# Cosine-similarity attention: reciprocal norms by a GpSimd power instead of Newton steps on VectorE

## The chip, the cores and the metric

One core of a Trainium2 chip. The metric is the device time of one run in microseconds (us), lower is better. Engines: PE (matrix products), DVE (VectorE), ACT (ScalarE), POOL (GpSimd), SP (issues DMAs). A difference of about 0.2% can be told from none.

## The reference

Eight batches of twelve heads, 512 tokens of 64 numbers each. Q and K are divided by their row norms, the scores are divided by tau = 0.1, and softmax weights multiply V.

```python
Q_norm = Q / (np.linalg.norm(Q, axis=-1, keepdims=True) + 1e-10)
K_norm = K / (np.linalg.norm(K, axis=-1, keepdims=True) + 1e-10)
scores = np.einsum('bhqd,bhkd->bhqk', Q_norm, K_norm) / tau
weights = np.exp(scores - np.max(scores, axis=-1, keepdims=True))
weights = weights / (np.sum(weights, axis=-1, keepdims=True) + 1e-10)
return np.einsum('bhqk,bhkd->bhqd', weights, V)
```

## The kernel before, in words

The 96 heads are taken as 48 pairs s = 0 to 47. Each operation is a node with a key, an engine, the nodes it needs and a function that issues it. `ORDER` lists, for each of the five engines, the keys in the order in which the engine issues them; the engines run these lists strictly in order and wait for one another by semaphores. So a node that waits holds up all that stand behind it on its engine. A key such as `SCL.4.1` is pair 4's product for K (0 is Q, 1 is K).

For a pair s the work is:

- `LD.s.0`, `LD.s.1`, `LV.s` (L379, L382): SP loads Q, K and V, 256 KB each, into rings of 18 (Q, K) and 6 (V) buffers. The first three K loads are on ACT's queue.
- `SQ.s.0` (L231): POOL squares Q and K together, 128x1024 in one instruction, into bf16. Pairs 0 to 2 are split between POOL and ACT.
- `SSQ.s` (L246) and `RED.s` (L253): PE adds groups of four columns by a product with the identity, DVE adds the rest. For eight pairs (`DIRECT`) DVE reduces the squares itself (L240).
- `NEW.g.k` (L349 to L368): pairs 2 and 3 are groups g of their own, from pair 4 on a group is two pairs. DVE works out the reciprocal norms from a bit-trick seed (L350) by two Newton steps: two times L341 and L342, and three times the form of L346, the last two for Q's and for K's result. That is eight instructions on at most 32 columns. The tiles are in PSUM (`nps`) and SBUF (`ys`, `rk`).
- `SCL.s.0` on DVE and `SCL.s.1` on POOL (both L270): Q and K times their reciprocal norms, 128x512 each, into bf16 `qn`. K of pairs 2 and 3 is on DVE.
- `TR.s` (L277) on PE turns `qn`, `EVA.s` (L421) on DVE copies it to `qt`. For seven pairs (`XT`) a DMA turns the K half (L416).
- `SCO.s.c` (L431), c = 0 to 3: scores of 128 keys by 512 queries for two heads, into one of two halves of `scps`. `SCO.s.c` waits until the exponential two steps back has read its half.
- `EXP.s.c` (L453): ACT takes the exponential of 128x1024 scores; since the norms are 1, no maximum is subtracted. Pair 0 has halves with a scale of its own (L443).
- `VC.s` (L458): POOL turns V into bf16, with a column of ones beside it.
- `PV.s.h.t` (L469), `RCP.s` (L481), `NRM.s` (L483), `ST.s` (L487): PE multiplies the weights by V, DVE divides by the sums, SP stores 256 KB. The last pair is done in three parts (L498 to L517).

Pairs 0 and 1 get their reciprocal norms from ACT (`LN`, `EX`, L259 and L263). `warm` and `fill` are matrix products without use that keep PE busy at the start (L218).

Of the kernel before, what the change touches and what calls it, by code (L numbers as in the profile page):

```python
# [5 lines left out]
ALU = mybir.AluOpType  # L6
# [119 lines left out]
def bass_cosine_similarity_attention_kernel(  # L126
# [12 lines left out]
    MAGIC = float(0x5F375A86)  # L139
    f32, bf16, i32 = mybir.dt.float32, mybir.dt.bfloat16, mybir.dt.int32  # L140
# [5 lines left out]
    def sb(name, shape, dt):  # L146
        return nc.alloc_sbuf_tensor(name, shape, dt)
# [11 lines left out]
    rk = [sb(f"rk{i}", [128, W], f32) for i in range(R_X)]  # L159
# [41 lines left out]
    def scores_read(s, c):  # L201
# [9 lines left out]
        compare_op=ALU.is_equal, fill=0.0))  # L211
    P.add("vone", "pool", ["eye"], lambda e: e.memset(  # L212
# [110 lines left out]
    def k_norms(g, i, j):  # L323

        tile = n_ps[:, g % R_X, 5 * W : 6 * W] if engine("pool", "SCL", first[g] + i, 1) == "dve" else rk[g % R_X][:, :]
        return tile[:, 8 * i : 8 * j]

    def k_runs(g):

        engs = [engine("pool", "SCL", first[g] + i, 1) for i in range(sizes[g])]  # L330
        cuts = [0] + [i for i in range(1, sizes[g]) if engs[i] != engs[i - 1]] + [sizes[g]]
        return list(zip(cuts, cuts[1:]))

    def norms(g):

        pairs = range(first[g], first[g] + sizes[g])
        m = 8 * sizes[g]
        xg = n_ps[:, g % R_X, 0 : 2 * m]
        tg = n_ps[:, g % R_X, 2 * W : 2 * W + 2 * m]
        yg = ys[g % R_X][:, 0 : 2 * m]  # L340
        yx = lambda e: e.tensor_tensor(out=tg, in0=xg, in1=yg, op=ALU.mult)  # L341
        yyx = lambda e: e.scalar_tensor_tensor(  # L342
            out=tg, in0=tg, scalar=-0.5, in1=yg, op0=ALU.mult, op1=ALU.mult)

        def up(dst, lo, hi):
            return lambda e: e.scalar_tensor_tensor(  # L346
                out=dst, in0=tg[:, lo:hi], scalar=1.5, in1=yg[:, lo:hi], op0=ALU.add, op1=ALU.mult)
# [7 lines left out]
        for k, step in enumerate(steps):  # L355
            if k:
                needs = [("NEW", g, k - 1)]
            else:
                needs = [("RED", i, w) for i in pairs for w in range(2) if ("RED", i, w) in P.ops]
            if k < 2:  # L360
                needs += [n for n in (("NEW", g - R_X, j) for j in range(6, 11)) if n in P.ops]
            if k == 6 and g >= R_X:
                needs += [("SCL", i, 0) for i in range(first[g - R_X], first[g - R_X] + sizes[g - R_X])]
            P.add(("NEW", g, k), "dve", needs, step)
        for k, (i, j) in enumerate(k_runs(g), 7):
            P.add(("NEW", g, k), "dve",
                  [("NEW", g, 5)] + ([("SCL", p, 1) for p in range(first[g - R_X], first[g - R_X] + sizes[g - R_X])] if g >= R_X else []),
                  up(k_norms(g, i, j), m + 8 * i, m + 8 * j))  # L368

    def pair(s):  # L370
# [55 lines left out]
        for c in range(NT):  # L426
            b = c % 2

            def sco(e, c=c, b=b):
                for h in range(2):  # L430
# [6 lines left out]
                  [("SCO", s, c - 1) if c else None, ("EVA", s), key("EVA", s, 1), key("XT", s),  # L437
# [99 lines left out]
ON = {'SQ.0.0.0': 'pool', 'SQ.0.0.1': 'act', 'SQ.0.1': 'act', 'SCL.0.1': 'pool', 'EVA.0.1': 'dve', 'SQ.1.0': 'pool', 'SQ.1.1': 'act', 'SCL.1.1': 'pool', 'SQ.2.0': 'pool', 'SQ.2.1': 'act', 'SCL.2.1': 'dve', 'SCL.3.1': 'dve'}  # L537
# [174 lines left out]
```

## Time and profile before

| | |
|---|---|
| Median of three runs | 194.41 us (194.25 to 194.46) |
| Span of the profiled execution, first to last instruction | 192.3 us |
| What the median has outside that span | 2.1 us |
| TensorE clock granted, mean | 0.995 |
| Exponentials of 128x1024 on ACT | 187, mean 1135 ns, overlapping |
| DMA moved | 51.71 MB, mean 269 GB/s |

For the profiled execution the profile gives the span; its own total time is not listed, so it is set against the runs by the difference in the third row. In the profile, a row such as "L270 POOL TENSOR_TENSOR ... x44 | 45.6, 1046 | 10.2" is a group of 44 instructions of line 270 on POOL, busy 45.6 us together, 1046 ns each, with 10.2 us of idle time ahead of them and behind the arrow what ended most of it. Rows of a timeline begin with the start and the length in us. A DMA row ends with the size and the us from issue to landing; one that comes from a narrow window has only the issue in that window.

### The profile page before, as it was taken

How to read it: one execution, taken by the hardware profiler on the slowest of the kernel's cores; microseconds unless marked ns; L12 is line 12 of the kernel's file. 1: busy time of each engine (PE TensorE's matmuls, PEld its weight loads, DVE VectorE, ACT ScalarE, POOL GpSimd, SP SyncE). 2: the span in 40 equal slices, each digit the busy share in tenths (PEclk: the TensorE clock that was granted, in tenths of full speed). 3: DMA queues.
4: the chain of work that ended last, by engine and by line, in shares of the span. 5: the costliest groups of instructions: out<-in, count | busy, mean ns of one | idle time of the engine just before them, and what ended most of it. 6: DMA issues, size and time to landing. Idle time of an engine off the chain costs nothing.

```text
span 192.3 us, 7111 instructions
## 1 busy us (share of the span) xinstructions
PE 179.5 (93%) x2944; PEld 117.6 (61%) x2944; DVE 148.3 (77%) x450; ACT 182.3 (95%) x210; POOL 161.8 (84%) x149
## 2 busy tenths in 40 slices
PE   7799999999998999999999899999999999999891
PEld 5466666656665565666666565666566656566560
DVE  1588887988888798868897887798888778976632
ACT  3599999999999999999999999999999999999990
POOL 4599899999999969999989988799999999927000
PEclk9999999999999999999999999999999999999998
DMA  5999999999999999989999999038799536650545
GB/s 185 360 349 349 352 336 321 373 251 344 341 376 303 374 364 332 314 251 310 364 346 339 285 376 387 16 88 254 242 254 356 130 109 197 193 136 3 182 148 165
DMA packets 56240, 51.71 MB, mean 269 GB/s; under 512 B 6928, under 2 KB 56208, under 8 KB 56208
## 3 DMA queue, kind: packets, MB, share of 16 engines
q1 hardware_dynamic: 55248, 50.41, 84.6%
q10 hardware_dynamic: 960, 0.85, 1.3%
q8 instruction: 23, 0.38, 0.9%
q14 instruction: 9, 0.07, 0.1%
HBM read 37.75 MB, written 12.58 MB: 262 GB/s over the span
## 4 chain that ended last, share of the span: by engine, by line
ACT 67%; POOL 15%; PE 8%; DMA 3%; DVE 2%; issue 2%; SPq 0%
ACT et L453 67%; POOL sq L231 8%; POOL qn L270 4%; DMA qk<-in_Q_dram 3%; POOL vb L458 3%; PE scps L431 2%; PE ops L469 2%; PE xps L246 2%; PE ops L218 1%; PE xps L277 1%; DVE ob L513 1%; PE nps L498 0%; SPq L294 0%; DVE ob L483 0%; POOL vb L212 0%
## 5 line engine op out<-in xcount | busy, mean ns | idle before, releaser
L453 ACT ACTIVATE et<-scps 128x1024 bf16<-128x1024 f32 x187 | 172.2, 1135 | 0.3
L231 POOL TENSOR_TENSOR sq<-qk 128x1024 bf16<-128x1024 f32 (+2 forms) x48 | 87.5, 1837 | 4.2 <-DMA qk<-in_Q_dram 4.2
L431 PE MATMUL scps<-qt 64*128 64x512 bf16 x384 | 74.7, 386 | 4.4 <-ACT et L453 2.4
L469 PEld LDWEIGHTS ops<-vb,et 128*128 128x128 bf16 x1504 | 53.4, 98 | 27.2 <-issue 22.2
L469 PE MATMUL ops<-vb,et 128*128 128x65 bf16 x1504 | 68.2, 194 | 0.6 <-DVE nps L341 0.4
L270 POOL TENSOR_TENSOR qn<-qk,rk 128x512 bf16<-128x512 f32 x44 | 45.6, 1046 | 10.2 <-DVE rk L346 10.2
L421 DVE COPY qt<-xps 128x1024 bf16<-128x1024 bf16 (+1 forms) x47 | 30.4, 647 | 3.7 <-PE xps L277 3.2
L483 DVE TENSOR_TENSOR ob<-ops,rd 128x512 f32<-128x512 f32 x47 | 32.4, 689 | 1.1
L270 DVE TENSOR_TENSOR qn<-qk,nps 128x512 bf16<-128x512 f32 x48 | 31.9, 680 | 0.3
L431 PEld LDWEIGHTS scps<-qt 64*128 64x128 bf16 x384 | 18.6, 92 | 20.3 <-ACT et L453 7.4
L458 POOL TENSOR_SCALAR vb<-vf 128x512 bf16<-128x512 f32 x48 | 29.7, 630 | 0.0
L277 PE MATMUL xps<-ident,qn 128*128 128x128 bf16 x352 | 27.9, 220 | 0.4 <-DVE qn L270 0.2
L246 PE MATMUL xps<-sq,ident 128*128 128x64 bf16 x624 | 24.9, 192 | 2.0 <-POOL sq L231 0.9
L277 PEld LDWEIGHTS xps<-ident,qn 128*128 128x128 bf16 x352 | 19.9, 98 | 10.4 <-issue 3.0
L246 PEld LDWEIGHTS xps<-sq,ident 128*128 128x128 bf16 x624 | 20.8, 97 | 8.9 <-issue 3.8
L481 DVE RECIPROCAL rd<-ops 128x8 f32<-128x8 f32 x47 | 9.7, 206 | 15.6 <-PE ops L469 15.2
L253 DVE TENSOR_REDUCE nps<-xps 128x16 f32<-128x64 f32 x38 | 8.8, 232 | 9.3 <-PE xps L246 8.9
L240 DVE TENSOR_REDUCE nps<-sq 128x8 f32<-128x512 bf16 x16 | 10.8, 684 | 0.0
L341 DVE TENSOR_TENSOR nps<-nps,ys 128x32 f32<-128x32 f32 (+1 forms) x48 | 9.3, 195 | 1.1
L342 DVE SCALAR_TENSOR_TENSOR nps<-nps,ys 128x32 f32<-128x32 f32 (+1 forms) x48 | 9.2, 193 | 1.0
L218 PE MATMUL scps<-warm_in 128*128 128x256 bf16 x28 | 5.8, 384 | 1.1 <-DVE warm_in L216 1.1
L218 PEld LDWEIGHTS scps<-warm_in 128*128 128x128 bf16 x28 | 3.7, 138 | 2.3 <-DVE warm_in L216 1.1
(42 smaller groups left out, 46.1 us busy)
## 6 DMA issues: line engine op xcount, KB each, us to landing
vf<-in_V_dram SPq DMA_DIRECT2D x48, 256.0 KB, 6.0
qk<-in_Q_dram SPq DMA_DIRECT2D x47, 256.0 KB, 6.0
out_dram<-ob SPq DMA_DIRECT2D x47, 256.0 KB, 5.3
qk<-in_K_dram SPq DMA_DIRECT2D x45, 256.0 KB, 6.0
qk<-in_K_dram ACTq DMA_DIRECT2D x3, 256.0 KB, 4.7
qk<-in_Q_dram SPq DMA_DIRECT2D x2, 128.0 KB, 2.7
out_dram<-ob SPq DMA_DIRECT2D x1, 128.0 KB, 2.3
qt<-qn SPq DMA_TRANSPOSE x7, 4.9
```

Source lines behind the costliest of these rows:

```text
L218: P.add(key, "pe", needs, lambda e: e.matmul(out=bank[:, 0:256], lhsT=warm_in[:, 0:128], rhs=warm_in[:, :], start=True, stop=True))
L231: emit = lambda e: e.tensor_tensor(out=b, in0=a, in1=a, op=ALU.mult)
L240: lambda e, w=w: e.tensor_reduce(out=dst(w), in_=sq[s % R_SQ][:, 8 * w : 8 * w + 8, :], axis=AX.X, op=ALU.add))
L246: last = e.matmul(out=x_ps[:, 0:64], lhsT=ident[:, :], rhs=sq[s % R_SQ][:, :, 4 * k : 4 * k + 4], start=(k == 0), stop=(k == 15))
L270: lambda e: e.tensor_tensor(out=qn[iqn][:, w].rearrange("p t h d -> p h t d"), in0=qk[iq][:, w].rearrange("p h (t d) -> p h t d", t=NT), i ...
L277: last = e.transpose(dst[:, i, :], qn[s % R_QN][:, b // NT, b % NT].rearrange("p h d -> p (h d)"), ident[:, :])
L421: lambda e: e.tensor_copy(out=qt[iqt][:, :].rearrange("p w t x -> p (w t) x")[:, 0:nb], in_=tb[:, 0:nb]))
L431: last = e.matmul(out=sc_ps[:, 2 * b + h, :], lhsT=qt[iqt][64 * h : 64 * h + 64, 1, c, :], rhs=qt[iqt][64 * h : 64 * h + 64, 0, :, :], sta ...
L453: lambda e, c=c, b=b: e.activation(out=et[iet][:, c, :, :], in_=sc_ps[:, 2 * b : 2 * b + 2, :], func=ACT.Exp, scale=inv_tau))
L458: lambda e: e.tensor_scalar(out=vb[:, iq, :, :, 0:DIM].rearrange("p c h d -> p h c d"), in0=vf[iv][:, :, :].rearrange("p h (c d) -> p h c ...
L469: last = e.matmul(out=o_ps[:, h, 65 * t : 65 * t + 65], lhsT=et[iet][:, c, h, 128 * t : 128 * t + 128], rhs=vb[:, iq, c, h, :], start=(c = ...
L483: lambda e: e.tensor_tensor(out=ob[io][:, :], in0=grid[:, :, :, 0:DIM], in1=rd[io][:, :].unsqueeze(3).to_broadcast([128, 2, NT, DIM]), op= ...
```

## The change

Four things change.

1. The Newton steps go. A group's sums are clamped from below by DVE into SBUF (`NEW.g.0`), POOL raises them to the power -0.5 in one instruction of at most 32 columns (`POW.g`, against a column of -0.5), and DVE copies the result to PSUM (`NEW.g.1`). The products of the group on DVE need the copy, a K product on POOL needs the power alone.
2. K's product of the odd pairs from 5 to 47 goes from POOL to DVE. Those of pairs 4, 6, and so on to 46 stay on POOL.
3. The order lists of all five engines are others.
4. The `fill` products get fixed places in their own chain: they are added ahead of the pairs, `SCO.0.1` names the ninth and the first `PV` the last of them. They run in PE's order, which the order list sets.

```diff
-        steps = [
-            lambda e: e.tensor_scalar(
-                out=yg.bitcast(i32), in0=xg.bitcast(i32), scalar1=-0.5, scalar2=MAGIC,
-                op0=ALU.mult, op1=ALU.add),
-            yx, yyx, up(yg, 0, 2 * m), yx, yyx,
-            up(n_ps[:, g % R_X, 4 * W : 4 * W + m], 0, m)]
...
+        P.add(("NEW", g, 0), "dve", needs + [key("POW", g - R_X)],
+              lambda e: e.tensor_scalar(out=yg, in0=xg, scalar1=TINY, scalar2=1.0, op0=ALU.max, op1=ALU.mult))
...
+        P.add(("POW", g), "pool", [("NEW", g, 0), "half", key("NEW", g - R_X, 1)] + gone,
+              lambda e: e.tensor_tensor(out=rg, in0=yg, in1=half[:, 0:1].to_broadcast([128, 2 * m]), op=ALU.pow))
...
+        P.add(("NEW", g, 1), "dve", [("POW", g)] + old,
+              lambda e: e.tensor_copy(out=n_ps[:, g % R_X, 2 * W : 2 * W + n], in_=rg[:, 0:n]))
...
+            rk, done = k_norms(g, i)
+            scaled(s, 0, "dve", n_ps[:, g % R_X, 2 * W + c8 : 2 * W + c8 + 8], [("NEW", g, 1)])
+            scaled(s, 1, engine("pool", "SCL", s, 1), rk, [done])
```

The first part of the orders, as far as the prediction speaks of it (the rest differs in the same way):

```diff
 "sp"
-        LD.0.0.0 LD.0.0.1 LD.1.0 LD.2.0 LV.0 LD.3.1 LD.3.0 LD.4.1 LD.4.0 LD.5.1 LD.5.0 LD.7.1 LV.1 LD.6.1 LD.6.0 LD.9.0
-        LD.7.0 LD.8.1 LV.2 LD.11.0 LV.4 LD.8.0 LD.13.1 LD.9.1 LV.3 LD.11.1 LV.6 LV.5 LV.7 LD.10.1 LV.8 LD.10.0 LD.17.0
-        LD.15.1 LD.16.1 LD.12.1 LD.13.0 LD.12.0 LD.14.1 ST.0 LD.18.0 LV.9 LD.14.0 LD.15.0 LD.16.0 LD.25.0 XT.9 ST.3
+        LD.0.0.0 LD.0.0.1 LD.1.0 LD.2.0 LV.0 LD.3.1 LD.4.0 LD.3.0 LD.9.1 LD.4.1 LD.9.0 LD.5.0 LD.6.0 LD.7.1 LD.5.1 LV.1
+        LD.6.1 LV.2 LD.10.0 LV.5 LV.3 LD.7.0 LD.11.0 LD.14.1 LD.8.0 LD.16.0 LD.8.1 LD.11.1 ST.0 LD.15.0 LV.4 LD.13.1
+        LD.14.0 LV.8 LD.10.1 LV.6 LD.15.1 LD.25.0 LV.9 LD.23.0 LD.19.0 LV.7 LD.12.1 LD.13.0 LD.19.1 LD.18.0 ST.1 LD.12.0
 "pool"
-        one eye SQ.0.0.0 SCL.0.1 SQ.1.0 vone SQ.2.0 SCL.1.1 VC.0 SQ.3.0 SQ.4.0 SQ.5.0 VC.1 SQ.6.0 SQ.7.0 SCL.4.1 VC.2
-        VC.4 SCL.5.1 SQ.9.0 VC.3 SQ.8.0 SCL.6.1 SQ.10.0 SCL.7.1 VC.5 SQ.11.0 SCL.9.1 SCL.8.1 VC.6 SQ.13.0 SQ.12.0 VC.7
+        one eye SQ.0.0.0 vone half SCL.0.1 SQ.1.0 SQ.2.0 VC.0 SCL.1.1 POW.0 SQ.3.0 SQ.4.0 POW.1 SQ.5.0 VC.1 SQ.6.0 POW.2
+        SQ.7.0 SCL.4.1 VC.2 VC.3 POW.3 SQ.9.0 SQ.8.0 SCL.6.1 VC.4 VC.5 POW.4 SQ.10.0 SQ.11.0 SCL.8.1 SQ.13.0 VC.6
+        SQ.12.0 POW.5 VC.7 SCL.10.1 SQ.15.0 VC.8 POW.6 SQ.14.0 VC.9 SCL.12.1 SQ.17.0 POW.7 VC.10 SCL.14.1 VC.11 SQ.16.0
 "dve"
+        wz RED.0.0.0 RED.0.0.1 SCL.0.0 RED.0.1 EVA.0 EVA.0.1 RED.1.0 RED.2.0 NEW.0.0 SCL.1.0 NEW.0.1 EVA.1 SCL.2.1
+        SCL.2.0 RED.3.0 NEW.1.0 EVA.2 NEW.1.1 SCL.3.0 RED.4.0 SCL.3.1 RED.5.0 NEW.2.0 RCP.0 NRM.0 EVA.3 NEW.2.1 RED.6.0
+        SCL.4.0 SCL.5.1 RCP.1 RED.7.0 NRM.1 NEW.3.0 EVA.4 SCL.5.0 NEW.3.1 RCP.2 NRM.2 EVA.5 SCL.6.0 SCL.7.0 RED.9.0
 "pe"
-        PV.0.0.1 PV.0.0.2 PV.0.0.3 PV.0.1.0 SCO.1.3 SSQ.4 SCO.2.0 PV.0.1.1 PV.0.1.2 PV.0.1.3 SSQ.5 SCO.2.1 TR.3 SCO.2.2
-        PV.1.0.0 SCO.2.3 PV.1.0.1 PV.1.0.2 SSQ.6 SCO.3.0 PV.1.0.3 PV.1.1.0 PV.1.1.1 SCO.3.1 PV.1.1.2 PV.1.1.3 SSQ.7
-        SCO.3.2 TR.4 SCO.3.3 PV.2.0.0 PV.2.0.1 PV.2.0.2 PV.2.0.3 SCO.4.0 PV.2.1.0 SCO.4.1 TR.5 PV.2.1.1 PV.2.1.2
+        PV.0.0.0 PV.0.0.1 PV.0.0.2 PV.0.0.3 PV.0.1.0 SCO.2.0 PV.0.1.1 SSQ.4 SCO.2.1 SSQ.5 SCO.2.2 PV.0.1.2 PV.0.1.3
+        SCO.2.3 TR.3 PV.1.0.0 PV.1.0.1 SCO.3.0 PV.1.0.2 PV.1.0.3 PV.1.1.0 SSQ.6 PV.1.1.1 SCO.3.1 SCO.3.2 PV.1.1.2
+        PV.1.1.3 SSQ.7 SCO.3.3 TR.4 PV.2.0.0 PV.2.0.1 PV.2.0.2 PV.2.0.3 PV.2.1.0 SCO.4.0 PV.2.1.1 PV.2.1.2 PV.2.1.3
 "act"
-        table LD.0.1 LD.1.1 LD.2.1 SQ.0.0.1 SQ.0.1 LN.0.0 EX.0.0 LN.0.1 SQ.1.1 EX.0.1 SQ.2.1 LN.1 EX.1.0 EX.1.1
+        LD.1.1 table LD.0.1 LD.2.1 SQ.0.0.1 LN.0.0 EX.0.0 SQ.0.1 SQ.1.1 SQ.2.1 LN.0.1 EX.0.1 LN.1 EX.1.1 EXP.0.0.0
```

At the end of the run `ST.47.0` stands ahead of `ST.47.1` on SP, the other way round before; the last part's store stays on ACT's queue.

More of the change, by code (lines that the diff above doesn't have):

```diff
@@ L211, in bass_cosine_similarity_attention_kernel @@
         compare_op=ALU.is_equal, fill=0.0))
+    P.add("half", "pool", [], lambda e: e.memset(half[:, :], -0.5))
     P.add("vone", "pool", ["eye"], lambda e: e.memset(
@@ L355, in norms @@
[L355 to L368, printed above, removed]
+        yg, rg = ys[g % R_X][:, 0 : 2 * m], rr[g % R_X][:, 0 : 2 * m]
+        needs = [("RED", i, w) for i in pairs for w in range(2) if ("RED", i, w) in P.ops]
+        P.add(("NEW", g, 0), "dve", needs + [key("POW", g - R_X)],
+              lambda e: e.tensor_scalar(out=yg, in0=xg, scalar1=TINY, scalar2=1.0, op0=ALU.max, op1=ALU.mult))
```

246 lines of the change are left out of this document (112 added, 134 removed).

## The prediction

> **What bounds the kernel now.** I read the page first: busy shares, then the 40 slices.
>
> ```profile
> span 192.3 us, 7111 instructions
> PE 179.5 (93%) x2944; PEld 117.6 (61%) x2944; DVE 148.3 (77%) x450; ACT 182.3 (95%) x210; POOL 161.8 (84%) x149
> ...
> ACT  3599999999999999999999999999999999999990
> POOL 4599899999999969999989988799999999927000
> ...
> DMA  5999999999999999989999999038799536650545
> ```
>
> ACT is full from the third slice to the tail. PE, POOL and, for the first half, the DMA engines are nearly full too, so whatever comes late there has little room to be made up. The chain of waits and ACT's timeline say how strictly ACT sets the end.
>
> ```profile
> 49.52 1.01 POOL qn L270
> 50.54 0.63 PE xps L246 x16
> ...
> 51.53 6.58 ACT et L453 x7
> ...
> 60.96 123.08 ACT et L453 x134
> ```
>
> ```profile
> 25.49 161.29 ACT L453 ACTIVATE et<-scps 128x1024 bf16<-128x1024 f32 x175
> 186.65 1.18 ACT L449 ACTIVATE et<-scps 128x512 bf16<-128x512 f32 x3
> 36.70 11.13 ACT L453 ACTIVATE et<-scps 128x1024 bf16<-128x1024 f32 x12
> 47.55 3.03 ACT L453 ACTIVATE et<-scps 128x1024 bf16<-128x1024 f32 x3
> L453 ACT ACTIVATE et<-scps 128x1024 bf16<-128x1024 f32 x187 | 172.2, 1135 | 0.3
> ```
>
> The rows are from windows that open at their first start. One exponential lasts 1.135, but they overlap: the twelve from 36.70 on take 10.85 until the next starts at 47.55, so the tightest spacing is 0.904. The 175 from 25.49, where pair 4 begins, to 186.65 take 0.921 each, or 3.68 a pair: small gaps cost 175 x 0.017 = 3.0 in all. Taking work off DVE and POOL can win at most that; the exponentials themselves stay, and whatever comes late to them is lost. Up to 50.5 the chain leads back through POOL, not ACT: early in the kernel POOL only just keeps ahead.
>
> **The change, part by part.**
>
> ```profile
> L231 POOL TENSOR_TENSOR sq<-qk 128x1024 bf16<-128x1024 f32 x45 | 84.7, 1897 | 0.0
> L270 POOL TENSOR_TENSOR qn<-qk,rk 128x512 bf16<-128x512 f32 x44 | 45.6, 1046 | 10.2 <-DVE rk L346 10.2
> L458 POOL TENSOR_SCALAR vb<-vf 128x512 bf16<-128x512 f32 x48 | 29.7, 630 | 0.0
> L270 DVE TENSOR_TENSOR qn<-qk,nps 128x512 bf16<-128x512 f32 x48 | 31.9, 680 | 0.3
> L341 DVE TENSOR_TENSOR nps<-nps,ys 128x32 f32<-128x32 f32 x44 | 8.6, 196 | 1.0
> L342 DVE SCALAR_TENSOR_TENSOR nps<-nps,ys 128x32 f32<-128x32 f32 x44 | 8.5, 194 | 0.9
> L346 DVE SCALAR_TENSOR_TENSOR ys<-nps,ys 128x32 f32<-128x32 f32 x22 | 4.1, 188 | 0.5
> L231 POOL TENSOR_TENSOR sq<-qk 128x256 bf16<-128x256 f32 x1 | 0.6, 613 | 1.9 <-DMA qk<-in_Q_dram 1.9
> ```
>
> *VectorE.* A group of two pairs loses eight Newton instructions of about 0.19 (two each of L341 and L342, the seed, three at L346): 1.5. It gains a clamp and a copy, 0.19 each by the same rows, and one product of 0.68: net -0.4 a group. DVE is at 77%, so I count nothing for it.
>
> *GpSimd.* POOL gives up 22 of its 44 products (22 x 1.04 = 23) and takes 24 powers, each of length p. No row shows a power. From below: POOL's two-operand rows of 256 and 1024 columns lie on 0.19 + 0.00167 x columns, so 32 columns cost 0.25 if a power costs what a multiply does. From above I allow what the 1024-column square takes, 1.9, that is 32 multiplies an element. A power needs a logarithm, a product and an exponential, so I take p = 1.0, nearest to the 128x512 product (1.046, 16 multiplies an element). Per two pairs, busy time over count gives squares 2 x 1.88, copies 2 x 0.62 and products 1.04: POOL needs 6.04 + p after, against 7.07 before, and ACT allows 8 x 0.921 = 7.37. So up to p = 1.3 POOL's throughput suffices, and at 1.0 it has as little to spare as now.
>
> The Trainium skill speaks against the move (GPSIMD Engine Reference, Elementwise - side-by-side cycle accounting): a GpSimd add of 2048 columns takes 4497 ns and GpSimd is about twice as slow as VectorE elementwise. By its rate 32 columns of add would be 0.07 us plus dispatch, an estimate below my lower end, with which the sum would not change; it prices no power. This trace's products of one shape, 1046 on POOL and 680 on DVE, agree in direction, at 1.5.
>
> *The added wait.* Each group now goes DVE clamp, POOL power, DVE copy. Behind the waiting copy on DVE stand the products of the group and the evacuations of qt (L399, L421 before); behind the power on POOL stand the squares. At p = 1.0 the order has other work between clamp and copy (for group 2 RCP.0, NRM.0 and EVA.3, the last two 1.4 by their rows below). I cost it at nothing; without that cover, up to p of it lands on ACT.
>
> ```profile
> L483 DVE TENSOR_TENSOR ob<-ops,rd 128x512 f32<-128x512 f32 x47 | 32.4, 689 | 1.1
> L421 DVE COPY qt<-xps 128x1024 bf16<-128x1024 bf16 x40 | 27.5, 687 | 3.3 <-PE xps L277 2.8
> ```
>
> *The load order.* This is where I see the time go. Pair 7's Q load is 17th on SP before and 22nd after; the 22 have the same bytes, and none waits. In the window around the 22nd issue of before:
>
> ```profile
> 14.48 0.67 SPq L379 DMA_DIRECT2D qk<-in_Q_dram  x1
> qk<-in_Q_dram SPq DMA_DIRECT2D x1, 256.0 KB, 8.2
> DMA packets 4692, 4.53 MB, mean 349 GB/s; under 512 B 280, under 2 KB 4691, under 8 KB 4691
> ```
>
> Issued at 14.48, landed 8.2 later: 22.7. Over 10 to 23 us the engines move 349 GB/s with every slice full, so no load overtakes. LD.7.0 lands at 22.7 after the change.
>
> *What waits for it.* POOL's order is now SQ.6.0, POW.2, SQ.7.0, SCL.4.1; before, SCL.4.1 ran at 21.89.
>
> ```profile
> 9.76 1.04 POOL L270 TENSOR_TENSOR qn<-qk,xr 128x512 bf16<-128x512 f32 x1 [0.20 <-ACT xr L263]
> 21.89 1.04 POOL L270 TENSOR_TENSOR qn<-qk,rk 128x512 bf16<-128x512 f32 x1 [0.64 <-DVE rk L346]
> 23.59 0.62 PE L277 MATMUL xps<-ident,qn 128*128 128x128 bf16 x8
> 24.24 0.69 DVE L421 COPY qt<-xps 128x1024 bf16<-128x1024 bf16 x1
> 25.05 0.39 PE L431 MATMUL scps<-qt 64*128 64x512 bf16 x2
> ```
>
> Pair 1's product still ends at 10.8 (VC.0 fits ahead of it). Then three powers, four squares and VC.1: 10.8 + 3.0 + 4 x 1.88 + 0.6 = 21.9, so POOL stands about 0.8 waiting for the load. From the landing: square 22.75 to 24.6, SCL.4.1 to 25.65, TR.4 0.62 to 26.3, EVA.4 0.69 to 27.0, SCO.4.0 0.39, and with some 0.03 at each handover EXP.4.0 starts at 27.5 instead of 25.49: **+2.0**. PE waits at SSQ.7 for the same square just ahead of SCO.3.3, so the cover that EXP.3.3 could give is gone too. Part of the 2.0 is lost earlier anyway: TR.3 now stands behind SCO.2.3, which must wait for EXP.2.1, and 1.135 + 0.39 + 0.62 + 0.69 + 0.39 = 3.2 from there to EXP.3.0 is 0.5 more than three spacings.
>
> *Head and tail.* K of pairs 0 and 1 change places on ACT's queue, but the exponentials still start behind LD.1.0 and SSQ.1; EX.1.0 moves into the stream, 0.1 earlier start, given back. The last store is still ACT's:
>
> ```profile
> 189.06 0.37 ACTq L517 DMA_DIRECT2D out_dram<-ob  x1
> out_dram<-ob ACTq DMA_DIRECT2D x1, 64.0 KB, 2.4
> ```
>
> so exchanging ST.47.0 and ST.47.1 changes nothing. Elsewhere on SP the new order puts waits earlier (the 38th entry now waits for SCL.7.0); a load is issued about 8 ahead of its landing by the row above, which covers a stand of two or three.
>
> *A second late load.* LD.12.0 is 48th on SP now. The 48th before:
>
> ```profile
> 38.09 0.58 SPq L487 DMA_DIRECT2D out_dram<-ob  x1
> out_dram<-ob SPq DMA_DIRECT2D x1, 256.0 KB, 3.7
> ```
>
> It landed at 41.8. SQ.12.0 to 43.7, SSQ.12 and SCO.8.3 about 1.0: EXP.8.3 at 44.8, against 27.5 + 19 x 0.904 = 44.7 with no gap. I add 0.1; one more full load ahead of it would make it 0.9.
>
> *The sum:* +2.1 on a span of 192.3 gives 194.4. The runs' median is 194.41, so 2.1 lies outside the span: **196.5**. The rest of the stream I leave at its 0.921.
>
> **Rivals.**
>
> *Faster: the gaps close.* If p is near 0.25, POOL's need falls from 7.07 to 6.3 a group and POOL runs ahead; gaps like that before 51.53, where the chain comes from POOL, vanish. Its place is the stream from pair 4 on, its price at most -3.0: 194.41 + 2.1 - 3.0 = 193.5. It outweighs the late load where the spacing falls under 0.909, and shows as faster under 0.907. Against it: from 60.96 on the chain runs in ACT alone, so most gaps are not POOL's.
>
> *The load is not late.* If LD.7.0 landed by 20.5, POOL would reach the square at 21.9 with p = 1.0, 0.85 less late: 195.6; with a short power TR.3's 0.5 would stay: 194.9. For it only that landings are read off another order; against it the full DMA slices.
>
> *The power is long.* POOL becomes the bound past p of 1.0 to 1.3. At 1.5: (7.54 - 7.37) x 22 groups = 4, and POOL reaches SQ.7.0 at 23.4, 0.6 after the load: 201. At 1.9: 0.57 x 22 = 13, and 1.8: 211. Nothing in the trace excludes it.
>
> *The first power loads code.* POOL would stand before POW.0; 0.8 of that is hidden by the wait for LD.7.0. The nearest first-use row is ACT's:
>
> ```profile
> 0.81 1.28 ACT L215 ACT_TABLE_LOAD   x1 [0.81 <-PEq L694]
> ```
>
> At 1.28 it adds 0.5: 197.0. The Trainium skill (GPSIMD Engine Reference, Instruction dispatch) gives about 6 us for the first call of a freshly loaded GpSimd kernel; as an estimate from that page it would add 5 and give 201.5, and no row here shows such a load. Against it: the first POOL square, 0.61, lies on the line of the later ones.
>
> **How the numbers follow.** Forecast 0.54 at 196.5 (own range 195.3 to 197.8: the second load, a gap or two more or fewer); long power 0.22, half of it under 202; gaps close 0.11; load not late 0.09; code load 0.04. A measurement of this kernel tells 0.2% (0.4 us) from no change. Of the gaps' 0.11, 0.07 is faster and 0.04 within 0.2%; of "load not late" 0.03 is within it, with a gap or two closed. So faster 0.07, same 0.07, slower 0.86. From 194.2 to 202.0 holds the forecast, load not late, code load, 0.03 of the gaps and half of the long power: 0.81.
>
> **What would show it.** POOL idle just under 1 us before the square of pair 7, released by qk from Q's load, and EXP.4.0 near 27.5: the load step. A power row near 1.0 or below: the p step; POOL at 9 in every slice and ACT idle throughout: the long power. Spacing under 0.910 after pair 4: the gaps. It is wrong if EXP.4.0 starts before 26, or if the powers' row is above 1.3.

## The result and the profile after

The changed kernel takes **302.7 us** (median of four runs, 301.3 to 304.4) against 194.4 for the kernel before in the same measurement: a ratio of **1.559, 95% interval 1.552 to 1.566**. Forecast were 196.5 us and a range of 194.2 to 202.0. The sign was right; nearly all of the size was missed. Where the executions of a kernel include disturbed ones, the ratios here leave these out and the medians don't, and the profiled executions of the short multiply and of the old loads, below, are disturbed ones.

The page of the changed kernel, the lines that answer to those shown of before:

```profile
span 299.5 us, 6971 instructions
PE 215.1 (72%) x2944; PEld 139.8 (47%) x2944; DVE 139.7 (47%) x328; ACT 190.7 (64%) x210; POOL 264.3 (88%) x152
...
ACT  4877159485468576757593456759646736680994
POOL 4799999999998999999999997999999999998000
PEclk9979579797798867959897776959789958695798
...
POOL 78%; PE 9%; issue 4%; ACT 4%; DVE 2%; DMA 1%; SPq 0%; POOLq 0%
```

ACT had 9 in every slice between head and tail; it now has holes throughout. POOL is the full one, and in the chain that ended last (the last line, shares of the span by engine) POOL takes the place that ACT had. The granted TensorE clock falls in many slices, to 0.825 on the mean. The groups of lines say what fills POOL and what ACT waits for (busy us, mean ns, then idle time ahead and its releaser):

```profile
L342 POOL TENSOR_TENSOR rr<-ys,half 128x32 f32<-128x32 f32 x22 | 119.4, 5425 | 5.3 <-DVE ys L339 2.8 <-PE scps L409 2.4
L342 POOL TENSOR_TENSOR rr<-ys,half 128x16 f32<-128x16 f32 x2 | 5.8, 2908 | 0.6 <-DVE ys L339 0.6
L232 POOL TENSOR_TENSOR sq<-qk 128x1024 bf16<-128x1024 f32 x45 | 84.6, 1893 | 0.0
L271 POOL TENSOR_TENSOR qn<-qk,rr 128x512 bf16<-128x512 f32 x22 | 22.9, 1042 | 0.3
L431 ACT ACTIVATE et<-scps 128x1024 bf16<-128x1024 f32 x187 | 180.2, 1030 | 99.1 <-PE scps L409 98.4
```

L342 is the power: **5.43 us on 32 columns**, 2.91 on 16. The square and the product last what they lasted before. ACT stands 98.4 us waiting for scores. The table of windows splits the span at the end of POOL's last instruction, first of the changed kernel, then of before (the sixth group of numbers is POOL's busy time):

```profile
0.00:276.00 276.00, 196.60 (x2662) 128.30 (x2662) 128.07 (x302) 172.60 (x189) 264.25 (x152) 0.82 0.58 178
276.00:299.50 23.50, 18.50 (x284) 11.47 (x282) 11.64 (x27) 18.05 (x21) 0.00 (x0) 0.86 0.34 108
```

```profile
0.00:177.40 177.40, 169.85 (x2780) 111.35 (x2781) 142.21 (x434) 171.93 (x198) 161.81 (x149) 1.00 0.90 278
177.40:192.30 14.90, 9.68 (x168) 6.21 (x166) 6.13 (x16) 10.42 (x14) 0.00 (x0) 0.94 0.48 160
```

This accounts for the whole 107.2 us between the spans. POOL's busy time grows by 102.4, which is 125.2 of powers less the 22.7 of products given up. Its idle time ahead of the last instruction falls from 15.6 to 11.8, by 3.8. What is still to be done when POOL has finished grows from 14.9 to 23.5, by 8.6.

In POOL's timeline of the changed kernel the powers stand between the squares with almost no idle time around them (start, duration):

```profile
11.66 2.92 POOL L342 TENSOR_TENSOR rr<-ys,half 128x16 f32<-128x16 f32 x1 [0.57 <-DVE ys L339]
...
18.25 2.90 POOL L342 TENSOR_TENSOR rr<-ys,half 128x16 f32<-128x16 f32 x1
...
25.41 5.42 POOL L342 TENSOR_TENSOR rr<-ys,half 128x32 f32<-128x32 f32 x1
30.80 1.89 POOL L232 TENSOR_TENSOR sq<-qk 128x1024 bf16<-128x1024 f32 x1
```

The last row is the square of pair 7. It has no wait for Q's load: POOL comes to it 8 us after the time (22.75) that the forecast had for its start.

### The profile page after: what moved, and what is told of

Its sections match the earlier page's. It is cut to its first block, busy times and chain, and to the rows that moved or that the text cites. A ratio compares the mean times of both kernels' runs of the same rounds, so it can differ in the third digit from the quotient of the medians.

```text
span 299.5 us, 6971 instructions
## 1 busy us (share of the span) xinstructions
PE 215.1 (72%) x2944; PEld 139.8 (47%) x2944; DVE 139.7 (47%) x328; ACT 190.7 (64%) x210; POOL 264.3 (88%) x152
## 4 chain that ended last, share of the span: by engine, by line
POOL 78%; PE 9%; issue 4%; ACT 4%; DVE 2%; DMA 1%; SPq 0%; POOLq 0%
POOL rr L342 42%; POOL sq L232 23%; POOL vb L436 8%; POOL qn L271 6%; ACT et L431 4%; PE scps L409 3%; PE ops L447 3%; PE xps L278 1%; PE xps L247 1%; DMA qk<-in_Q_dram 1%; DVE qn L271 1%; PE scps L219 1%; DVE ob L491 0%; DVE ob L461 0%; DVE qt L399 0%
## 5 line engine op out<-in xcount | busy, mean ns | idle before, releaser
L431 ACT ACTIVATE et<-scps 128x1024 bf16<-128x1024 f32 x187 | 180.2, 1030 | 99.1 <-PE scps L409 98.4
L342 POOL TENSOR_TENSOR rr<-ys,half 128x32 f32<-128x32 f32 (+1 forms) x24 | 125.2, 5215 | 5.9 <-DVE ys L339 3.3
L447 PE MATMUL ops<-vb,et 128*128 128x65 bf16 x1504 | 82.1, 211 | 35.0 <-DVE ob L461 23.9
L447 PEld LDWEIGHTS ops<-vb,et 128*128 128x128 bf16 x1504 | 65.6, 109 | 68.3 <-issue 27.2
L409 PE MATMUL scps<-qt 64*128 64x512 bf16 x384 | 85.7, 446 | 3.9 <-ACT et L431 2.1
L278 PE MATMUL xps<-ident,qn 128*128 128x128 bf16 x352 | 34.1, 251 | 19.2 <-DVE qn L271 12.8
L271 DVE TENSOR_TENSOR qn<-qk,nps 128x512 bf16<-128x512 f32 x70 | 46.3, 677 | 0.2
L247 PE MATMUL xps<-sq,ident 128*128 128x64 bf16 x624 | 30.6, 210 | 21.3 <-POOL sq L232 12.3
L346 DVE COPY nps<-rr 128x32 f32<-128x32 f32 (+1 forms) x24 | 4.6, 193 | 78.8 <-POOL rr L342 78.8
L247 PEld LDWEIGHTS xps<-sq,ident 128*128 128x128 bf16 x624 | 26.2, 109 | 30.8 <-POOL sq L232 16.1
L278 PEld LDWEIGHTS xps<-ident,qn 128*128 128x128 bf16 x352 | 24.8, 112 | 30.8 <-DVE qn L271 14.3
L271 POOL TENSOR_TENSOR qn<-qk,rr 128x512 bf16<-128x512 f32 x22 | 22.9, 1042 | 0.3
```

The costliest lines, as they stand in the source:

```text
L247: last = e.matmul(out=x_ps[:, 0:64], lhsT=ident[:, :], rhs=sq[s % R_SQ][:, :, 4 * k : 4 * k + 4], start=(k == 0), stop=(k == 15))
L271: lambda e: e.tensor_tensor(out=qn[iqn][:, w].rearrange("p t h d -> p h t d"), in0=qk[iq][:, w].rearrange("p h (t d) -> p h t d", t=NT), i ...
L278: last = e.transpose(dst[:, i, :], qn[s % R_QN][:, b // NT, b % NT].rearrange("p h d -> p (h d)"), ident[:, :])
L342: lambda e: e.tensor_tensor(out=rg, in0=yg, in1=half[:, 0:1].to_broadcast([128, 2 * m]), op=ALU.pow))
L409: last = e.matmul(out=sc_ps[:, 2 * b + h, :], lhsT=qt[iqt][64 * h : 64 * h + 64, 1, c, :], rhs=qt[iqt][64 * h : 64 * h + 64, 0, :, :], sta ...
L431: lambda e, c=c, b=b: e.activation(out=et[iet][:, c, :, :], in_=sc_ps[:, 2 * b : 2 * b + 2, :], func=ACT.Exp, scale=inv_tau))
```

## The experiments

The first theory, **A**: the length of the power on POOL's queue makes the loss. Rivals: **B**, the waiting of VectorE for GpSimd and back costs, not the length; **C**, the lower TensorE clock or shared memory traffic costs. Beside that stood the forecast's own load term, which the power hides.

### The power replaced by a short multiply

```diff
-    P.add("half", "pool", [], lambda e: e.memset(half[:, :], -0.5))
+    P.add("half", "pool", [], lambda e: e.memset(half[:, :], 1.0 / 512))
...
-              lambda e: e.tensor_tensor(out=rg, in0=yg, in1=half[:, 0:1].to_broadcast([128, 2 * m]), op=ALU.pow))
+              lambda e: e.tensor_tensor(out=rg, in0=yg, in1=half[:, 0:1].to_broadcast([128, 2 * m]), op=ALU.mult))
```

> The changed kernel with the power's one instruction turned into a multiply of the same 128x32 tile by 1/512 (so the norms are not computed: every row is scaled by its sum of squares over 512, a value near a true reciprocal norm for these inputs). GpSimd's queue, the wait from clamp to product, the K products on VectorE and all orders stay. Theory A (the length of the power is nearly all of the loss): the instruction falls from 5.42 us to about 0.25, GpSimd needs 6.04 + 0.25 = 6.3 us per two pairs against ScalarE's 7.37, and the time comes back to 194-197 us. Rival B (the round trip VectorE - GpSimd - VectorE makes it, whatever the instruction lasts): stays above 250 us. Rival C (TensorE's lower clock or shared memory traffic of the new order makes it): stays well above 200 us, with the clock near 0.83. Within theory A: if the later load of pair 7's Q costs the 2.0 us of the forecast, 196.5 and the first exponential of pair 4 at 27.5 us; if it costs nothing, 194.4 and 25.5 us.

Measured: 198.34 us, ratio 1.0193 (1.015 to 1.0235). Queue, waits, K products and orders are those of the changed kernel; only the length went, from 5.4 to 0.24 us, and with it 104 of the 108 us. B and C fall as explanations of the bulk: the wait chain is all there, and the clock is back at 0.98 or more. What is left, 1.9% or 3.7 us, is more than zero, and more than the forecast's 2.1 us.

### The multiply at the forecast's length, and at its upper bound

```diff
+    wide = [sb(f"wide{i}", [128, 16, 2 * W], f32) for i in range(R_X)]
+    rr = [x[:, 0] for x in wide]
...
-              lambda e: e.tensor_tensor(out=rg, in0=yg, in1=half[:, 0:1].to_broadcast([128, 2 * m]), op=ALU.pow))
+              lambda e: e.tensor_tensor(
+                  out=wide[g % R_X][:, :, 0 : 2 * m], in0=yg.unsqueeze(1).to_broadcast([128, 16, 2 * m]),
+                  in1=half[:, 0:1].unsqueeze(2).to_broadcast([128, 16, 2 * m]), op=ALU.mult))
```

> As the multiply in place of the power, but over 512 columns (16 copies of the 32), so that it lasts about 0.19 + 512 x 0.00167 = 1.05 us: the length at which the forecast was made (norms not computed here either). Theory A: GpSimd needs 6.04 + 1.05 = 7.1 us per two pairs against 7.37, so the time is the same as with the short multiply within 0.5 us, 194.4-197 us; the forecast's own figure is 196.5. If single waits behind this instruction matter already at 1 us, it is 1-3 us longer than the short multiply.

Measured: 200.82 us, ratio 1.0334 (1.0286 to 1.0381). At 1.04 us the time is 2.7 us longer than at 0.24, not the same within 0.5: the length costs something before POOL's sum is full. Which waits make the 2.7 us is not located. The forecast's 196.5 is some 4 us short even at the p that it took. The second length, with 33 copies in place of 16, 1056 columns:

> A multiply over 33 copies of the 32 columns (1056, about 1.95 us) in place of the power (norms not computed): the length of the forecast's upper bound for the power. The forecast's formula gave 211 us at 1.9. The runs so far give 200.4 us at a mean length of 1.01 and 245.4 at 3.01, 22.5 us for each us: a straight line gives 220 at 1.9 (mean over the 24). If GpSimd becomes the bound only from 1.33 us on (6.04 + p = 7.37), the line is bent and the time 210-216.

Measured: 218.63 us, ratio 1.1266 (1.1216 to 1.1315). The forecast's formula (211) is too low, the straight line (220) nearly right. So the turn, an estimate from these runs, lies near 1.0 us and not at 1.33: from 0.24 to 1.04 us a us of length costs 3.4 us of time, from there to 1.94 some 20. Here the row is 1.94 us; the second line below is ACT's slices, with holes spread over the whole run.

```profile
L343 POOL TENSOR_TENSOR wide<-ys,half 128x1056 f32<-128x1056 f32 x22 | 42.7, 1942 | 2.0 <-PE scps L412 1.8
```

```profile
ACT  3699779998899989999999759999969999939992
```

### The power on half the columns

```diff
-              lambda e: e.tensor_tensor(out=rg, in0=yg, in1=half[:, 0:1].to_broadcast([128, 2 * m]), op=ALU.pow))
+              lambda e: (e.tensor_tensor(out=rg[:, 0:m], in0=yg[:, 0:m], in1=half[:, 0:1].to_broadcast([128, m]), op=ALU.pow),
+                         e.tensor_scalar(out=rg[:, m : 2 * m], in0=yg[:, m : 2 * m], scalar1=1.0 / 512, scalar2=1.0, op0=ALU.mult, op1=ALU.mult))[1])
```

> The changed kernel with the power on half of its columns (16 of 32: Q's norms) and a multiply by 1/512 on the other half (so K's norms are not computed). Theory A (length, by the column): the power's row reads 2.9 us at 16 columns in the changed kernel, so p = 2.9 + 0.2 = 3.1; each us of p costs about 23 us of time where GpSimd is the bound (22 groups of two pairs and two of one), so 302.7 - (5.4 - 3.1) x 23 = 250 us (245-255). A rival in which the power costs its time per instruction, whatever its size, gives about 300 us.

Measured: 245.4 us, ratio 1.2638 (1.2584 to 1.2691), inside the expected 245 to 255. Its two groups of powers:

```profile
L342 POOL TENSOR_TENSOR rr<-ys,half 128x16 f32<-128x16 f32 x22 | 64.0, 2908 | 4.0 <-DVE ys L339 2.2 <-PE scps L410 1.7
L342 POOL TENSOR_TENSOR rr<-ys,half 128x8 f32<-128x8 f32 x2 | 3.3, 1654 | 1.0 <-DVE ys L339 1.0
```

8, 16 and 32 columns take 1.654, 2.908 and 5.425 us: a line, 0.40 + 0.157 x columns. So the cost is by the column, with 0.40 us for the instruction itself.

### No power, its length made of multiplies

```diff
+        P.add(("LONG", g), "pool", [("NEW", g, 0), "half", key("LONG", g - 1)],
+              lambda e: e.tensor_tensor(
+                  out=wide[:, :, 0 : 2 * m], in0=yg.unsqueeze(1).to_broadcast([128, 94, 2 * m]),
+                  in1=half[:, 0:1].unsqueeze(2).to_broadcast([128, 94, 2 * m]), op=ALU.mult))
...
-              lambda e: e.tensor_tensor(out=rg, in0=yg, in1=half[:, 0:1].to_broadcast([128, 2 * m]), op=ALU.pow))
+              lambda e: e.tensor_tensor(out=rg, in0=yg, in1=half[:, 0:1].to_broadcast([128, 2 * m]), op=ALU.mult))
 "pool"
-        SQ.6.0 POW.2
+        SQ.6.0 LONG.2 POW.2
```

> The changed kernel without a power: a multiply over 94 copies of the 32 columns (3008), whose result nobody reads, takes its place for about 0.19 + 3008 x 0.00167 = 5.2 us, and a multiply by 1/512 over 32 columns gives the factors (norms not computed). Together 5.45 us, the length of the power. Theory A (the time on GpSimd's queue alone): the time of the changed kernel, 300-306 us, and TensorE's granted clock as low as there. If the power does something beside taking its time (a slower memory port, a clock of its own), it is shorter than that by what this is worth.

Measured: 300.53 us, ratio 1.5505 (1.5428 to 1.5582), clock 0.831.

```profile
L343 POOL TENSOR_TENSOR wide<-ys,half 128x3008 f32<-128x3008 f32 x22 | 114.5, 5205 | 5.6 <-DVE ys L340 2.9 <-PE scps L414 2.5
L347 POOL TENSOR_TENSOR rr<-ys,half 128x32 f32<-128x32 f32 x22 | 5.4, 244 | 0.0
```

Plain multiplies that hold POOL for 5.45 us give the changed kernel's time, and its low clock too. So the power does nothing beside taking its time: theory A, with no remainder that the intervals show. The low clock comes with the length of POOL's work, whatever that work is; it is no cause of its own.

### The power unread

```diff
-              lambda e: e.tensor_tensor(out=rg, in0=yg, in1=half[:, 0:1].to_broadcast([128, 2 * m]), op=ALU.pow))
+              lambda e: e.tensor_tensor(out=rg, in0=yg, in1=small[:, 0:1].to_broadcast([128, 2 * m]), op=ALU.mult))
+        P.add(("SPARE", g), "pool", [("NEW", g, 0), "half", key("SPARE", g - 1)],
+              lambda e: e.tensor_tensor(out=spare[:, 0 : 2 * m], in0=yg, in1=half[:, 0:1].to_broadcast([128, 2 * m]), op=ALU.pow))
 "pool"
-        SQ.6.0 POW.2
+        SQ.6.0 POW.2 SPARE.2
```

> The changed kernel in which a multiply by 1/512 over 32 columns gives the factors (norms not computed) and the power follows it at once on GpSimd, into a tile that nobody reads. VectorE's copy and the products wait only for the short multiply; GpSimd is held for 0.25 + 5.4 us. Theory A: GpSimd's queue is the bound, so at most a few us are won: 300-308 us. Rival B (VectorE's wait for the power is what costs): back to 195-210 us.

Measured: 295.23 us, ratio 1.52 (1.5148 to 1.5252), below the expected 300 to 308: 7.6 us are won by the ratios (5.3 by the spans of the profiled runs) although POOL has 4.6 us more to do. The windows of this run say where:

```profile
0.00:276.20 276.20, 200.05 (x2710) 128.52 (x2711) 132.18 (x309) 176.28 (x194) 268.88 (x177) 0.82 0.57 179
276.20:294.20 18.00, 13.46 (x236) 8.84 (x236) 7.84 (x20) 14.05 (x18) 0.00 (x0) 0.94 0.37 123
```

POOL ends where it did (276.2 against 276.0) with 268.9 us of work in place of 264.3, so it stands less. The work after that falls from 23.5 to 18.0 us: copy and VectorE's products come a power earlier, and TensorE's clock there is 0.94 in place of 0.86. These two are not separated. By the spans, the waiting for the power is worth the 5.3 us won and the 4.6 of added work taken in: B is true for some 10 us of 107, about one power's length of it at the end.

### The load of pair 7, moved in the kernel before

```diff
-        LD.7.0 LD.8.1 LV.2 LD.11.0 LV.4 LD.8.0 LD.13.1
+        LD.8.1 LV.2 LD.11.0 LV.4 LD.8.0 LD.7.0 LD.13.1
```

> The kernel before, whole, with one token moved: the load of pair 7's Q is issued 22nd on SyncE instead of 17th. If the forecast's load term is right, the squares of pair 7 start near 22 us instead of 19.4, pair 4's first exponential comes some 2 us later, and the time is 195.5-196.5 us (1.008-1.011 of before). If the load has slack there, within 0.3 us of before.

Measured: 196.98 us, ratio **1.0144 (1.0116 to 1.0171)**: 2.8 us, more than the 2.0 of the forecast, and a little above the expected 195.5 to 196.5. POOL's and ACT's timelines of this run:

```profile
22.20 1.89 POOL L231 TENSOR_TENSOR sq<-qk 128x1024 bf16<-128x1024 f32 x1 [3.12 <-DMA qk<-in_Q_dram]
```

```profile
25.33 1.02 ACT L453 ACTIVATE et<-scps 128x1024 bf16<-128x1024 f32 x1 [1.91 <-PE scps L431]
26.85 1.02 ACT L453 ACTIVATE et<-scps 128x1024 bf16<-128x1024 f32 x1 [0.49 <-PE scps L431]
28.38 2.85 ACT L453 ACTIVATE et<-scps 128x1024 bf16<-128x1024 f32 x3 [0.51 <-PE scps L431]
```

POOL waits 3.1 us for the load, and ACT loses 1.9 + 0.5 + 0.5 = 2.9 and never wins it back. One token five places down a DMA queue costs 1.4% of the kernel.

### The late loads moved forward in the new order

With the old list of SyncE as a whole:

```diff
 "sp" (short multiply), and on to its end
-        LD.0.0.0 LD.0.0.1 LD.1.0 LD.2.0 LV.0 LD.3.1 LD.4.0 LD.3.0 LD.9.1 LD.4.1 LD.9.0 LD.5.0 LD.6.0 LD.7.1 LD.5.1 LV.1
+        LD.0.0.0 LD.0.0.1 LD.1.0 LD.2.0 LV.0 LD.3.1 LD.3.0 LD.4.1 LD.4.0 LD.5.1 LD.5.0 LD.7.1 LV.1 LD.6.1 LD.6.0 LD.9.0
...
```

> As the short multiply, with SyncE's order of the kernel before (pair 7's Q is the 17th transfer issued there instead of the 22nd); norms not computed here either. If the forecast's load term is right (+2.0 us), 194.5 us, some 2 us below the short multiply with the new order, and the first exponential of pair 4 near 25.5 us. If that load hides nothing, the same as the short multiply within 0.4 us. The old list meets the other engines' new lists unsearched, so a loss elsewhere of up to 2 us is possible; the start of pair 4's first exponential separates the two.

Measured: 208.56 us, ratio 1.0715 (1.0667 to 1.0764): a miss, 10 us slower. In its trace POOL stands 15.8 us in eight places for V loads and 6.6 us once for a K load, and ACT 14.9 us in all for scores. The old list doesn't fit the other four, so it can't test the load term. Then single tokens, first two:

```diff
 "sp" (short multiply)
-    LD.6.1 LV.2 LD.10.0 LV.5 LV.3 LD.7.0 ... LV.7 LD.12.1 LD.13.0 LD.19.1 LD.18.0 ST.1 LD.12.0
+    LD.7.0 LD.6.1 LV.2 LD.10.0 LV.5 LV.3 ... LD.12.0 LV.7 LD.12.1 LD.13.0 LD.19.1 LD.18.0 ST.1
```

> The short multiply in place of the power (norms not computed), with two loads moved forward on SyncE: Q of pair 7 from 22nd to 17th, Q of pair 12 from 48th to 42nd. The short multiply as it stood was at 1.019 of before. Its trace shows two losses of ScalarE: 2 us ahead of pair 4's first exponential and 2.9 us in pair 8, whose scores stand on TensorE behind the sums of squares of pair 12. If the late loads make them: 1.019 falls to about 1.003-1.008 (0.6 us back at pair 4, where the old loads gave that much, and 2-2.9 us at pair 8). If something else in the orders makes them, it stays at 1.015-1.02.

Measured: 197.05 us, ratio 1.0142 (1.0107 to 1.0177). Less came back than the late loads should have given, and POOL's timeline shows why: with pair 12's load early, Q of pair 13 is the late one.

```profile
41.07 1.89 POOL L232 TENSOR_TENSOR sq<-qk 128x1024 bf16<-128x1024 f32 x1 [3.05 <-DMA qk<-in_Q_dram]
42.93 0.63 POOL L436 TENSOR_SCALAR vb<-vf 128x512 bf16<-128x512 f32 x1
43.52 1.89 POOL L232 TENSOR_TENSOR sq<-qk 128x1024 bf16<-128x1024 f32 x1
```

```diff
 "sp" (beside the two)
-    LD.25.0 LV.9 LD.23.0 LD.19.0 LD.12.0 LV.7 LD.12.1 LD.13.0
+    LD.12.0 LD.12.1 LD.13.0 LD.25.0 LV.9 LD.23.0 LD.19.0 LV.7
```

> The short multiply (norms not computed) with four loads moved forward: Q of pair 7 to 17th as in the two moved loads, and Q of 12, K of 12 and Q of 13 together from the places 43 to 48 to 38 to 40. With two moved loads ScalarE still lost 2.2 us in pair 8, and GpSimd's square of pair 13 began at the landing of Q of 13 (41.0 us). If the late loads are all of this loss, it goes: the square of pair 13 starts near 39 us, ScalarE waits under 0.5 us in pair 8, and the ratio falls from 1.014 to 1.002-1.007. If the loss stays, it is the place of the sums of squares ahead of the scores on TensorE.

Measured: 194.62 us, ratio **1.002 (0.9992 to 1.0048)**. POOL's timeline has the same two squares (of pairs 13 and 12) without a wait, 3 us earlier:

```profile
38.09 1.89 POOL L232 TENSOR_TENSOR sq<-qk 128x1024 bf16<-128x1024 f32 x1
39.95 0.63 POOL L436 TENSOR_SCALAR vb<-vf 128x512 bf16<-128x512 f32 x1
40.54 1.89 POOL L232 TENSOR_TENSOR sq<-qk 128x1024 bf16<-128x1024 f32 x1
```

So four loads standing late on SP are what the change costs beside the length of the power, as far as these runs can tell. And with these mended and the norms nearly free, the kernel is level with before, not faster.

### Transposes one place earlier

```diff
 "pe" (beside the two loads)
-    SCO.2.3 TR.3 ... SSQ.7 SCO.3.3 TR.4
+    TR.3 SCO.2.3 ... SSQ.7 TR.4 SCO.3.3
```

> As the two moved loads, and on TensorE the transposes of pairs 3 and 4 one place earlier, ahead of the last scores of pairs 2 and 3 (norms not computed). With the old loads ScalarE still waited 0.47 + 0.36 us in pair 3 and 0.38 us ahead of pair 4's first exponential, where these transposes stand behind scores. If their place makes that, 0.8-1.2 us (0.4-0.6%) below the two moved loads, and level with before, 0.998-1.004; if the transposes then hold the scores up, the same or up to 1 us longer.

Measured: 198.35 us, ratio 1.0234 (1.019 to 1.0279): no gain, rather a loss of 0.9% (the interval lies above that of the two moved loads). ACT's stand ahead of pair 4 moves into pair 3 (0.36 and 0.38 us) and doesn't go. The forecast's reason for the half microsecond there (a transpose behind scores) isn't confirmed. Why the time rose is left open: the profiled execution is the fastest of the six (195.74 us) and doesn't show the loss.

### Newton steps in the new orders, and K's product alone in the old ones

```diff
 "dve" (and so for every group; the steps are those of before)
-        RED.5.0 NEW.2.0 RCP.0 NRM.0 EVA.3 NEW.2.1 RED.6.0
+        RED.5.0 NEW.2.0 NEW.2.1 NEW.2.2 NEW.2.3 NEW.2.4 NEW.2.5 RCP.0 NRM.0 EVA.3 NEW.2.6 NEW.2.7 NEW.2.8 RED.6.0
 "pool"
-        SQ.6.0 POW.2
+        SQ.6.0
```

> The change without its first part: the Newton steps of the kernel before on VectorE at the places of clamp and copy, no power on GpSimd, with K's product of every second pair on VectorE and all the new orders. Theory A: without the power nothing of the 108 us is left; VectorE has 148 + 22 x 0.68 = 163 us of work, so 194-200 us. Rivals B and C: B also expects the loss gone here, but C (clock, order) expects it to stay well above 200 us.

Measured: 211.4 us, ratio 1.0912 (1.0875 to 1.0949), above the expected 194 to 200. The clock is 0.995 in the same orders, against C. But the orders were laid for two short VectorE instructions at these places; now six stand in a block where the clamp was and two or three where the copy was. ACT waits 13.4 us in 18 places for scores, and among PE's waits the largest is 9.5 us in 11 places for VectorE's output products (`ob`). That the blocks make these waits is argued, not tried by itself.

```diff
 ON (the kernel before)
+    'SCL.5.1': 'dve', 'SCL.7.1': 'dve', ... 'SCL.47.1': 'dve'
 "dve"
-    SCL.5.0 ...
+    SCL.5.0 SCL.5.1 ...
```

> The kernel before with the second part of the change alone: K's product of every second pair from pair 5 on stands on VectorE right behind Q's product of the pair, Newton steps and all other orders as before. VectorE has 148 + 22 x 0.7 = 163 us of work in 192, GpSimd 162 - 23 = 139. If ScalarE stays the bound, 194 us, within 0.5 of before; where the product delays VectorE's next step in a queue that was searched for other work, 194.5-200 us. Nothing near the changed kernel's 302.7 by any theory.

Measured: 196.75 us, ratio 1.0122 (1.0072 to 1.0172). VectorE gets the 22 products and one more short norm instruction a group. POOL has 22 us less to do, and ahead of its products it stands 28.3 us, 26.4 of them waiting for norms from VectorE (10.2 in the kernel before):

```profile
L270 POOL TENSOR_TENSOR qn<-qk,rk 128x512 bf16<-128x512 f32 x22 | 23.0, 1044 | 28.3 <-DVE nps L346 15.0 <-DVE rk L346 11.4 <-PE xps L277 1.9
```

The room won on POOL is worth nothing here. In this run ACT stands 1.6 us for scores and its exponentials begin 0.75 us later (14.96 against 14.21); the rest of the 2.8 us between the spans is not located.

## Why the prediction was wrong, point by point

**The step that failed: "so I take p = 1.0".** The power's length was bounded from above by "what the 1024-column square takes, 1.9, that is 32 multiplies an element"; it is 5.43, and by the slope it costs 0.157 against a multiply's 0.00167 us a column, 94 multiplies an element. No row of before showed a power, no run shows how GpSimd works one out, and an end taken from another instruction's row was no bound. It was the one open price that decided the sign of POOL's balance, and the range took in only half of the rival that turned on it. The rival "the power is long" named the mechanism, POOL as the bound with 9 in every slice and ACT idle throughout, and that is what came; its prices ended at 1.9. That the sign came out right is luck in so far as the forecast's own reason for it, the late load, costs nothing in the changed kernel.

**The formula for a long power** was right in form and too mild. It was (6.04 + p - 7.37) x 22 and a later head. At 5.43 it gives 90, and with 8 for POOL's later arrival at pair 7 (as measured) and 2 for the load 100; measured 107.2. The chain of waits has the last power, and what follows it (start, duration):

```profile
268.90 5.39 POOL rr L342
...
274.32 0.19 DVE nps L346
274.51 0.60 DVE qn L271
...
283.31 8.38 ACT et L431 x9
```

From the power at 25.41 to this one the distance is (268.90 - 25.41) / 21 = 11.6 each, against 6.04 + 5.43 = 11.47: POOL's need was well read. What it lacks is the longer tail, 8.6 us. Near the turn it lacks more: 211 at 1.9 against 218.6 measured at 1.94, and at p = 1.04 a time of 200.8 where it had nothing left over. "So up to p = 1.3 POOL's throughput suffices" holds for the sum of POOL's work; but POOL also stands for loads, 7.6 us for Q and K in the run at 1.04 (its waits below: in total, times, longest). Of these 2.1 lie ahead of 7 us, in the head, and 5.5 behind it, and 22 x 0.29 us of slack is 6.4. That the turn comes early for this reason is worked out, not tried by itself.

```profile
POOL sq L233 <- DMA qk<-in_Q_dram: 5.9, 5, 1.8
POOL sq L233 <- DMA qk<-in_K_dram: 1.7, 2, 1.2
```

**The load order, +2.0: the late square came as forecast; the account of what it costs was right only in part.** With p = 1.04, POOL waits 1.29 us for Q of pair 7 (forecast: just under 1), and pair 4's first exponential starts at 27.60 (forecast: 27.5), by POOL's and ACT's timelines of that run:

```profile
22.74 1.89 POOL L233 TENSOR_TENSOR sq<-qk 128x1024 bf16<-128x1024 f32 x1 [1.29 <-DMA qk<-in_Q_dram]
...
44.40 1.89 POOL L233 TENSOR_TENSOR sq<-qk 128x1024 bf16<-128x1024 f32 x1 [1.75 <-DMA qk<-in_Q_dram]
```

```profile
25.69 1.02 ACT L434 ACTIVATE et<-scps 128x1024 bf16<-128x1024 f32 x1 [0.54 <-PE scps L412]
27.60 2.85 ACT L434 ACTIVATE et<-scps 128x1024 bf16<-128x1024 f32 x3 [0.89 <-PE scps L412]
...
47.48 4.71 ACT L434 ACTIVATE et<-scps 128x1024 bf16<-128x1024 f32 x5 [2.17 <-PE scps L412]
```

Not all of the delay at pair 4 is the load's. From pair 1's first exponential to pair 4's it takes 11.28 us before (14.21 to 25.49), 13.70 here (13.90 to 27.60) and still 12.55 with the short multiply and the four loads moved forward (15.04 to 27.59), where ACT's timeline keeps three stands:

```profile
22.97 1.02 ACT L431 ACTIVATE et<-scps 128x1024 bf16<-128x1024 f32 x1 [0.47 <-PE scps L409]
24.36 2.85 ACT L431 ACTIVATE et<-scps 128x1024 bf16<-128x1024 f32 x3 [0.36 <-PE scps L409]
27.59 3.77 ACT L431 ACTIVATE et<-scps 128x1024 bf16<-128x1024 f32 x4 [0.38 <-PE scps L409]
```

In the short multiply's own trace, where Q of pair 7 is late still and POOL stands 1.39 us for it, it takes 12.56 (15.92 to 28.48) with the same three stands: there the exponentials begin 2 us later than in the run at 1.04 us, and the load shows no cost at pair 4. So by these single traces 1.3 of the 2.4 us are not the load's. The forecast had 0.5 for a transpose behind scores; moving the transposes did not take it away, and the cause is open. What the load can have cost here is the other 1.1.

In the changed kernel itself pair 7's load costs nothing, because POOL is late by more: the square runs at 30.8. The **second late load** was set at +0.1. ACT stands 2.2 us there, the last row of the timeline at 1.04 us: pair 12's square, whose sums stand on PE ahead of pair 8's last scores, starts on the landing at 44.4 and not at 41.8. The price was taken from the 48th transfer of before, a store that landed 3.7 us after its issue. This load was issued at 36.91, earlier than that, and took 7.4 us:

```profile
36.91 0.74 SPq L360 DMA_DIRECT2D qk<-in_Q_dram  x1
...
qk<-in_Q_dram SPq DMA_DIRECT2D x1, 256.0 KB, 7.4
```

The place on SP was right; the landing was read off a queue in another state. The new list has loads of pairs as late as 19, 23 and 25 ahead of it.

**The added wait, cost at nothing:** in the changed kernel DVE's copy waits 78.8 us in all for the power, by its row; the unread power shows the price, some 10 us by the spans. At the forecast's length the cover was nearly there: in the run at 1.04 us the copy waits 3.3 us, in four places.

```profile
L346 DVE COPY nps<-rr 128x32 f32<-128x32 f32 (+1 forms) x24 | 4.6, 193 | 78.8 <-POOL rr L342 78.8
L271 DVE TENSOR_TENSOR qn<-qk,nps 128x512 bf16<-128x512 f32 x70 | 46.3, 677 | 0.2
```

**VectorE, counted at nothing:** confirmed in the changed kernel; DVE's busy time falls from 148.3 to 139.7. That K's product on VectorE is harmless holds only for orders laid for it: in the old ones it cost 1.2%.

**The load is not late:** fell; POOL stood 1.29 us for it at p = 1.04. **The gaps close:** fell. With norms nearly free and the loads mended the ratio is 1.002, and in that trace the 175 exponentials from 27.59 to 189.05 take 0.923 each, where the forecast asked for less than 0.910: a freer POOL doesn't bring ACT's exponentials closer together. **The first power loads code:** fell. The first power takes 2.92 us and the second 2.90, by the timeline above, and nothing stands before it but the clamp. The Trainium skill (GPSIMD Engine Reference, Instruction dispatch) gives some 6 us for the first call of a freshly loaded kernel; this power shows nothing of the kind. The Trainium skill's elementwise rate (GPSIMD Engine Reference, Elementwise - side-by-side cycle accounting), from which the forecast worked out 0.07 us for 32 columns, is a rate for adds; for the power the trace says 5.43.

No version beats the kernel before: of every length tried for the reciprocal norm, down to 0.24 us, the best is level with it.

## What to carry to other kernels

An operation that no row shows, moved onto an engine at 84%, has no upper bound until it is measured: work out first at which length it makes that engine the bound (here about 1 us), and let the range take in lengths far beyond. In a full DMA queue, one load moved five places down made its reader stand 3.1 us and cost 2.8 us, and with ACT full nothing of that came back. Orders laid for one set of durations aren't neutral for another, so a part undone inside them, or an old list set among new ones, tells about the fit as much as about the part.

## What the runs showed of the hardware

GpSimd's power of two f32 operands costs 0.40 + 0.157 us a column (128 partitions): 1.65, 2.91 and 5.43 at 8, 16 and 32 columns. A multiply takes 0.24 at 32 columns and 5.2 at 3008. VectorE's and ScalarE's rows beside it don't lengthen: VectorE's product takes 677 ns against 680 (the row above), and the exponentials' mean even falls, from 1135 to 1030, as they no longer overlap. TensorE's granted clock falls from 0.995 with PE busy 93% to 0.825 at 72%, whether powers or multiplies make it wait (0.831). But the share of busy time alone doesn't set it: at 86% the profiled run with Newton steps kept 0.995, with no wait of PE above 1.3 us, while the run at 1.94 us had 0.966, with one of 2.8, and the run with the old loads, at 88%, had 0.964, with one of 5.7. That the length of the single waits decides is what these three suggest; no run tried it by itself.
